# The first norm of a two-layer decoder trunk: which engine forms its shifts, scales and sums of squares, and how many weight tiles follow its channel blocks

## The chip, the cores and the metric

The kernel runs on one core of a Trainium2 chip. The metric is device time in microseconds (us), the median of three runs. Engines are named as in the profile: PE is TensorE's matrix multiply, PEld its weight load, DVE is VectorE, ACT is ScalarE, POOL is GpSimd, SP is the queue from which all DMAs here are issued.

## The reference

There are two layers over 256 tokens of 1024 channels. Each has a mixer and an expert channel mixer, both behind a norm whose shift and scale come from a conditioning vector `c`. What matters here is the start of layer 0:

```
c_act = silu(c)
sh1, sc1, ... = split(c_act @ ada_w[0] + ada_b[0], 6)
h = x * rsqrt(mean(x*x) + 1e-6) * g * (1 + sc1) + sh1
z = h @ w_in          # mLSTM q, k, gates, o; MoBA q, k (column tiles); both v (row tiles)
```

`h` has 1024 channels, `w_in` gives 21 column tiles of 128 outputs and 8 row tiles for the two values. Everything after this is the same before and after the change.

## The kernel before

All work is float32. Channels are cut in eight blocks `kd` of 128, with channels on partitions and 256 tokens along the free axis. A weight tile is 128 x 1024 (512 KB); `load` (L146) takes it through SP into one of eight `raw` buffers. `split` (L152) makes a high part `hi` on ACT (L159) and a remainder `lo` on DVE (L162); three pairs of such buffers exist in the pool `stream`. A column tile against `h` then costs three matmuls of 256 columns for each channel block (`hi` by `hhi`, `hi` by `hlo`, `lo` by `hhi`: L185 to L187), 24 in all, which add up in one PSUM bank. We call such a sum over one weight tile a *tile product*.

`setup` (L85) loads the small parameters and `x`, forms `cact = silu(c)`, and copies `cact` to all partitions with eight f32 matmuls (L133); the result is `crow`.

`mixer0` (L426) begins with the norm. `norm_stat` (L271) squares one channel block on ACT (L279) and adds it to a running sum on DVE (L281); after the eighth, two f32 matmuls against a column of ones (L290) give the sum of squares per token. `norm_rstd` (L296) takes the power -1/2 on POOL (L262) and spreads the result over partitions with two f32 matmuls (L306). DVE then multiplies `x` by it (L440): `xn`.

For each channel block, `ada` (L244) forms 128 scales and then 128 shifts. Each is one custom DVE instruction over a 128 x 1024 tile of `ada_w` (L252), a read of its accumulator, and for the scale a small product (L255). ACT applies scale and shift twice (L449 gives `hhi`, L450 a float32 copy), DVE subtracts (L451 gives `hlo`). At blocks 4, 5 and 7 (`EARLY`) the first three column tiles are loaded and split. `col_tiles` (L189) multiplies those three in a staggered order through `mm_col` (L174), then goes on tile by tile, with a row step (12 matmuls of 512 columns, L237 to L239) behind some of them (`ROWS0`).

Each finished tile product is read from PSUM at once: the gates by DVE (L570, L571), a q or k tile by one ACT instruction (L484) and three on DVE (L486). The first nine column tiles are one of gates and eight of q and k.

The order of each engine's instructions is fixed ahead of the run by a planner. It takes the instructions in program order of priority, places each when its own cost table says that the inputs are there, and so may interleave products of several blocks; on the chip each engine works through its list in that order. `issue_after` holds an instruction behind another. `keep_warm` (L264) issues matmuls of 512 columns whose result nobody reads.

Of the kernel before, what the change touches and what calls it, by code (L numbers as in the profile page):

```python
# [9 lines left out]
F32 = mybir.dt.float32  # L10
# [10 lines left out]
P = 128  # L21
# [29 lines left out]
SIDE_N = ((8, 24), (0, 8))  # L51
EARLY = (4, 5, 7)
V1_AT = 15
# [21 lines left out]
class Prog:  # L75
# [9 lines left out]
    def setup(self):  # L85
# [35 lines left out]
        c = self.small[:, Cols.c:Cols.c + 8]  # L121
        cact = self.tmp.tile([P, KD], F32, tag="t8b", name="cact")
        e = self.tmp.tile([P, KD], F32, tag="t8", name="c_exp")
# [5 lines left out]
        for half in range(2):  # L129
            ps = self.psum("h")  # L130
            for k in range(4):
                kd = 4 * half + k
                nc.tensor.matmul(ps[:, k * P:(k + 1) * P], lhsT=cact[:, kd:kd + 1].to_broadcast([P, P]), rhs=self.ident,  # L133
                                 start=True, stop=True)
            self.last_crow = nc.vector.tensor_copy(self.crow[:, 512 * half:512 * half + 512], ps)

# [14 lines left out]

    def split(self, raw, late=None):  # L152

        nc = self.nc
        hi = self.stream.tile([P, 1024], F32R, tag="hi", name="hi")
        lo = self.stream.tile([P, 1024], F32R, tag="lo", name="lo")

        def high():
            nc.scalar.copy(hi, raw)  # L159

        def low():
            self.last_lo = nc.vector.tensor_tensor(out=lo, in0=raw, in1=hi.bitcast(F32), op=ALU.subtract)  # L162

        for part, kd in zip((high, low), late or (None, None)):
            if kd is None:
                part()
            else:
                self.late.append((kd, part))
        return hi, lo
# [18 lines left out]

    def col_tiles(self, aps, act, tags, kds=range(KD), ws=None, rest=None):  # L189

        n = len(tags)
        ws = ws or [self.wsplit(a) for a in aps[:n]]
        pss = [self.psum(t)[:, :T] for t in tags]
        self.mm_col(pss, ws, act, kds)
        yield from enumerate(pss)
        for i, a in enumerate(aps[n:]):
            ps = self.psum(rest(n + i) if rest else "h")[:, :T]
            w = self.take(a)
            self.mm_col([ps], [w], act)
            yield n + i, ps  # L200
# [62 lines left out]

    def keep_warm(self, n):  # L264

        ps = self.psum("h")
        for i in range(n):
            self.nc.tensor.matmul(ps, lhsT=self.zero.to_broadcast([P, P]), start=True, stop=True,
                                  rhs=self.iota.unsqueeze(1).to_broadcast([P, 4, P]))
# [61 lines left out]
    def alibi(self, pool):  # L331

        nc = self.nc
        di = pool.tile([P, T], I32, tag="sm_p", name="dist_i", bufs=12)
        nc.gpsimd.iota(di, pattern=[[-1, T]], base=P, channel_multiplier=1)
        df = pool.tile([P, T], F32, name="dist_f")
        nc.vector.tensor_copy(df, di)
        nc.gpsimd.affine_select(df, df, pattern=[[-1, T]], base=P, channel_multiplier=1, compare_op=ALU.is_ge, fill=-NEG)
        return df, pool.tile([P, NH, T], F32, name="alibi")

# [85 lines left out]
    def mixer0(self):  # L426
        nc, tc = self.nc, self.tc
        with ExitStack() as st:
# [3 lines left out]
            hlo = self.hp.tile([P, KD, T], F32R, tag="x", name="hlo")  # L432
            with tc.issue_after(self.last_crow.ins):
                for kd in range(KD):
                    self.norm_stat(kd, (0, 0))
            r = self.norm_rstd()
            xn = pool.tile([P, KD, T], F32, tag="yhi", name="xn")
            for half in range(2):
                ks = slice(4 * half, 4 * half + 4)
                nc.vector.tensor_mul(xn[:, ks, :], self.xT[:, ks, :], r.unsqueeze(1).to_broadcast([P, 4, T]))  # L440
            ws = []
            for kd in range(KD):
                for _ in chain(self.ada(0, 1, (kd,)), self.ada(0, 0, (kd,))):
                    pass
                if kd in EARLY:
                    ws.append(self.wsplit(self.io["ev_in"][(12, 0, 1)[len(ws)]]))
                g, sh = self.gsc[:, 0, 0, kd:kd + 1], self.mod[:, 0, kd:kd + 1]
                t = self.tmp.tile([P, T], F32, tag="nt", name="ht")
                nc.scalar.activation(hhi[:, kd, :], xn[:, kd, :], AF.Identity, bias=sh, scale=g)  # L449
                nc.scalar.activation(t, xn[:, kd, :], AF.Identity, bias=sh, scale=g)  # L450
                nc.vector.tensor_tensor(out=hlo[:, kd, :], in0=t, in1=hhi[:, kd, :].bitcast(F32), op=ALU.subtract)  # L451
            h = (hhi, hlo)
            yhi = pool.tile([P, KD, T], F32R, tag="yhi", name="yhi")
            ylo = pool.tile([P, KD, T], F32R, name="ylo")
            w_in = self.io["ev_in"]
            live = []

            qk = pool.tile([P, 8, T], F32, name="qk")
            mo = pool.tile([P, 4, T], F32, name="mo")
            cols = [12] + list(range(8)) + [13, 17, 14, 18, 15, 19, 16, 20, 8, 9, 10, 11]  # L460
            mv = pool.tile([P, TT, 4, P + 1], F32, name="mv")
            nc.vector.memset(mv[:, :, :, P:], 1.0)
            bv = pool.tile([P, TT, 1, 512], F32, name="bv")
            rows = {}
            zs = []
            cols = [w_in[c] for c in cols]
            row_aps = [self.io["ev_v"][n, w4] for n in range(2) for w4 in range(4)]
            self.feed, n = [], 0
            for i in range(3, 21):
                self.feed.append(cols[i])  # L470
                self.feed += row_aps[n:n + ROWS0.get(i, 0)]
                n += ROWS0.get(i, 0)
# [3 lines left out]
            tag0 = lambda i: "t" if min(ROWS0) < i <= max(ROWS0) else "h"  # L476
            for i, ps in self.col_tiles(cols, h, ("h", "h", "l"), ws=ws, rest=tag0):
                if i == 0:
# [41 lines left out]
            while live:  # L520
                self.advance(live)
            yield from self.residual(0, 16, self.io["ev_out"], (yhi, ylo), (4, 5, 6, 0, 1, 2, 3, 7))

    def moba_pair(self, pool, hp, zs, bv, bias, yhi, ylo):
# [628 lines left out]
def layout(x, c, ada_w, ada_b, norm_mix_g, norm_ffn_g, ev_w_in, ev_conv_w, ev_igate_b, ev_fgate_b, ev_mnorm_g,  # L1153
# [12 lines left out]
    def cols(v):  # L1166
# [12 lines left out]
    w = np.asarray(ev_w_in)[0]  # L1179
    z = lambda n: np.zeros((D, n), w.dtype)  # L1180
    gates = np.concatenate([w[:, 2048:2052], z(28), w[:, 2052:2056], z(92)], axis=1)
    ev = np.concatenate([w[:, 0:1024], w[:, 1536:2048], gates, w[:, 2056:3080]], axis=1)
# [3 lines left out]
        "small": np.ascontiguousarray(small),  # L1186
        "ada_w": np.ascontiguousarray(np.asarray(ada_w).transpose(0, 2, 1)).reshape(2, 6, KD, P, D),
        "ev_in": coltiles(ev),
        "ev_v": rowtiles(np.concatenate([w[:, 1024:1536], w[:, 3080:3592]], axis=1)),
# [28 lines left out]
```

## Time and profile before

| | |
|---|---|
| median of 3 runs | 1979.51 us (1978.45 to 1979.65) |
| the profiled execution: time / span | 1977.66 us / 1975.9 us |
| PE busy | 1934.8 us (98%), 13229 matmul instructions |
| DVE busy | 1538.6 us (78%) |
| ACT busy | 1136.1 us (57%) |
| granted clock of PE, mean | 0.989 |

Busy time is the share of the span in which an engine had an instruction in flight. An f32 matmul shows as two instructions, called passes below, and a matmul's shown duration overlaps with the next one's, so the cost of one in a stream is the distance between starts. [...]

### The profile page before, as it was taken

How to read it: one execution, taken by the hardware profiler on the slowest of the kernel's cores; microseconds unless marked ns; L12 is line 12 of the kernel's file. 1: busy time of each engine (PE TensorE's matmuls, PEld its weight loads, DVE VectorE, ACT ScalarE, POOL GpSimd, SP SyncE). 2: the span in 40 equal slices, each digit the busy share in tenths (PEclk: the TensorE clock that was granted, in tenths of full speed). 3: DMA queues.
4: the chain of work that ended last, by engine and by line, in shares of the span. 5: the costliest groups of instructions: out<-in, count | busy, mean ns of one | idle time of the engine just before them, and what ended most of it. 6: DMA issues, size and time to landing. Idle time of an engine off the chain costs nothing.

```text
span 1975.9 us, 34938 instructions
## 1 busy us (share of the span) xinstructions
PE 1934.8 (98%) x13229; PEld 1754.6 (89%) x13229; DVE 1538.6 (78%) x3336; ACT 1136.1 (57%) x2137; POOL 50.7 (3%) x37
## 2 busy tenths in 40 slices
PE   5999999999999999999999999999999999999999
PEld 4888999999999888888878799999999998888887
DVE  8977999789998666777578789988899975556655
ACT  4655555778775444444456554567877744444443
POOL 0020000000000000000012100000000000000000
PEclk7999999999999999999989999999999999999999
DMA  9863355444445666998356243554544455669660
GB/s 338 290 207 130 108 178 188 162 160 160 164 155 173 210 216 219 336 342 299 129 197 206 72 138 119 184 180 153 166 156 162 160 180 192 193 197 359 225 200 22
DMA packets 103992, 376.45 MB, mean 191 GB/s; under 512 B 11536, under 2 KB 12944, under 8 KB 103696
## 3 DMA queue, kind: packets, MB, share of 16 engines
q1 hardware_dynamic: 103824, 374.22, 56.3%
q8 instruction: 104, 1.70, 0.3%
q14 instruction: 64, 0.52, 0.1%
HBM read 373.12 MB, written 1.05 MB: 189 GB/s over the span
## 4 chain that ended last, share of the span: by engine, by line
PE 79%; DVE 12%; issue 5%; DMA 2%; ACT 1%; POOL 0%; POOLq 0%; ACTq 0%; DVEq 0%; SPq 0%
PE ps_h L185 12%; PE ps_acc L920 12%; PE ps_acc L921 12%; PE ps_acc L919 12%; PE ps_h L186 11%; PE ps_h L187 11%; DVE lo L162 4%; PE ps_g L1109 3%; DVE raw L252 1%; DMA raw<-in_ada_w_dram 1%; PE ps_l L389 1%; DVE idxs L987 1%; DVE mr L985 1%; DVE A L1116 1%; DVE idxs L984 1%
## 5 line engine op out<-in xcount | busy, mean ns | idle before, releaser
L159 ACT CAST hi<-raw 128x1024 fp32r<-128x1024 f32 x613 | 643.2, 1050 | 658.1 <-PE ps_acc L920 308.2
L162 DVE TENSOR_TENSOR lo<-raw,hi 128x1024 fp32r<-128x1024 f32 x613 | 748.3, 1221 | 300.7 <-ACT hi L159 297.7
L185 PE MATMUL ps_h<-h2hi,hi 128*128 128x256 f32 x2256 | 652.8, 289 | 1.1 <-ACT A L967 0.7
L187 PE MATMUL ps_h<-h2hi,lo 128*128 128x256 f32 x2256 | 638.3, 283 | 0.0
L186 PE MATMUL ps_h<-h2lo,hi 128*128 128x256 f32 x2256 | 638.1, 283 | 0.0
L185 PEld LDWEIGHTS ps_h<-h2hi,hi 128*128 128x128 f32 x2256 | 432.1, 192 | 2.0 <-ACT A L967 1.2
L187 PEld LDWEIGHTS ps_h<-h2hi,lo 128*128 128x128 f32 x2256 | 432.3, 192 | 0.9 <-DVE lo L162 0.4
L186 PEld LDWEIGHTS ps_h<-h2lo,hi 128*128 128x128 f32 x2256 | 432.9, 192 | 0.0
L919 PE MATMUL ps_acc<-hi,act 128*128 128x512 f32 x1024 | 397.8, 389 | 2.0 <-ACT act L900 2.0
L920 PE MATMUL ps_acc<-hi,act 128*128 128x512 f32 x1024 | 398.6, 389 | 0.1
L921 PE MATMUL ps_acc<-lo,act 128*128 128x512 f32 x1024 | 398.6, 390 | 0.0
L919 PEld LDWEIGHTS ps_acc<-hi,act 128*128 128x128 f32 x1024 | 192.1, 188 | 41.8 <-ACT act L900 2.4
L920 PEld LDWEIGHTS ps_acc<-hi,act 128*128 128x128 f32 x1024 | 192.2, 188 | 40.8 <-DVE act L901 1.0
L921 PEld LDWEIGHTS ps_acc<-lo,act 128*128 128x128 f32 x1024 | 192.0, 188 | 40.5 <-DVE lo L162 0.3
L252 DVE CUSTOM_DVE_ANT_0 raw<-raw,crow,small 128x1024 f32<-128x1024 f32 x96 | 122.6, 1279 | 26.6 <-DMA raw<-in_ada_w_dram 26.6
L1116 DVE SCALAR_TENSOR_TENSOR A<-A,ps_g 128x256 f32<-128x256 f32 (+28 forms) x214 | 124.4, 582 | 11.9 <-PE ps_g L1109 11.1
L1118 ACT ACTIVATE A<-ps_g 128x256 f32<-128x256 f32 (+39 forms) x170 | 69.2, 446 | 76.0 <-DVE A L1116 75.0
L1096 DVE TENSOR_TENSOR og<-oj,gt 128x512 f16<-128x512 f16 x256 | 100.8, 419 | 13.3 <-PE ps_g L1109 13.1
L1083 ACT ACTIVATE oi<-iota,in 128x128 f16<-128x128 f16 x320 | 107.1, 394 | 0.0
L185 PE MATMUL ps_h<-hhi,hi 128*128 128x256 f32 x248 | 76.0, 308 | 7.4 <-ACT hhi L449 3.4
L1109 PE MATMUL ps_g<-oi,og 128*128 128x128 f16 x1024 | 81.8, 223 | 0.0
L901 DVE TENSOR_TENSOR act<-A,act 128x1024 fp32r<-128x1024 f32 x64 | 78.0, 1218 | 1.5 <-ACT act L900 1.5
(313 smaller groups left out, 2076.1 us busy)
## 6 DMA issues: line engine op xcount, KB each, us to landing
raw<-in_uT_dram SPq DMA_DIRECT2D x256, 512.0 KB, 3.5
raw<-in_v_dram SPq DMA_DIRECT2D x256, 512.0 KB, 4.4
raw<-in_ada_w_dram SPq DMA_DIRECT2D x96, 512.0 KB, 5.1
raw<-in_wq_dram SPq DMA_DIRECT2D x32, 512.0 KB, 3.7
raw<-in_ev_in_dram SPq DMA_DIRECT2D x21, 512.0 KB, 5.0
raw<-in_od_in_dram SPq DMA_DIRECT2D x16, 512.0 KB, 4.3
raw<-in_ev_v_dram SPq DMA_DIRECT2D x8, 512.0 KB, 4.9
raw<-in_ev_out_dram SPq DMA_DIRECT2D x8, 512.0 KB, 4.5
```

The lines of the kernel that those rows point to most:

```text
L159: nc.scalar.copy(hi, raw)
L162: self.last_lo = nc.vector.tensor_tensor(out=lo, in0=raw, in1=hi.bitcast(F32), op=ALU.subtract)
L185: nc.tensor.matmul(ps, lhsT=whi[:, s], rhs=ahi[:, kd, :], start=kd == kds[0], stop=False)
L186: nc.tensor.matmul(ps, lhsT=whi[:, s], rhs=alo[:, kd, :], start=False, stop=False)
L187: nc.tensor.matmul(ps, lhsT=wlo[:, s], rhs=ahi[:, kd, :], start=False, stop=kd == kds[-1])
L252: nc.vector.tensor_tensor_reduce(w, w, self.crow, 1.0, self.small[:, ab:ab + 1], ALU.mult, ALU.add, m)
L919: nc.tensor.matmul(acc[q], lhsT=xhi, rhs=vhi[:, c], start=m == 0, stop=False)
L920: nc.tensor.matmul(acc[q], lhsT=xlo, rhs=vhi[:, c], start=False, stop=False)
L921: nc.tensor.matmul(acc[q], lhsT=xhi, rhs=vlo[:, c], start=False, stop=m == NEXP - 1)
L1083: nc.scalar.activation(oi[:, k, :], self.iota, AF.Square, bias=tabs["in"][:, t0 + k:t0 + k + 1])
L1109: nc.tensor.matmul(pv[:, k, :], lhsT=og[:, w, :, k], rhs=oi[:, k, :], start=w == 0, stop=w == 1)
L1116: nc.vector.scalar_tensor_tensor(dst, dst, 1.0 / GSC, pv[:, :, lo:m], op0=ALU.mult, op1=ALU.mult)
```

## The change

The work before the first tile products moves to a new function, `first_blocks`.

- The eight shifts, and the scales of channel blocks 1, 3, 5 and 7, are formed on PE: eight f32 matmuls with a weight tile as stationary operand and one column of `cact` as the moving one. They read a second copy of the same weights, `ada0`, laid out by column tiles. DVE adds the bias from PSUM. The other four scales stay on DVE. All twelve results go to columns of one PSUM tile, `sums`.
- The squares stay on ACT; PE sums them, two f32 matmuls of one column for each channel block, in place of DVE's additions.
- Six column tiles, instead of three, are loaded early. Tile products take a channel block as soon as `h` has it; a tile that comes later catches up. The pairs of buffers of tiles 3 to 5 lie in the room of tiles that are used later.
- Six, four and three matmuls of `keep_warm` stand behind the columns of blocks 0, 1 and 2.
- The six finished products are then read in the old order, and the rest goes on as before.

```diff
@@ -49,7 +49,9 @@
-EARLY = (4, 5, 7)
+SC_PE = (1, 3, 5, 7)
+FIRST = {0: 1, 1: 2, 2: 1, 3: 1, 4: 1}
+WARM0 = {0: 6, 1: 4, 2: 3}
@@ -119,7 +121,7 @@
-        cact = self.tmp.tile([P, KD], F32, tag="t8b", name="cact")
+        self.cact = cact = const.tile([P, KD], F32, name="cact")
@@ -132,7 +134,7 @@
-            self.last_crow = nc.vector.tensor_copy(self.crow[:, 512 * half:512 * half + 512], ps)
+            nc.vector.tensor_copy(self.crow[:, 512 * half:512 * half + 512], ps)
@@ -149,11 +151,10 @@
-    def split(self, raw, late=None):
-
-        nc = self.nc
-        hi = self.stream.tile([P, 1024], F32R, tag="hi", name="hi")
-        lo = self.stream.tile([P, 1024], F32R, tag="lo", name="lo")
+    def split(self, raw, late=None, parts=None):
+        nc = self.nc
+        hi, lo = parts or [self.stream.tile([P, 1024], F32R, tag=t, name=t) for t in ("hi", "lo")]
@@ -186,12 +187,13 @@
-    def col_tiles(self, aps, act, tags, kds=range(KD), ws=None, rest=None):
-
-        n = len(tags)
-        ws = ws or [self.wsplit(a) for a in aps[:n]]
-        pss = [self.psum(t)[:, :T] for t in tags]
-        self.mm_col(pss, ws, act, kds)
+    def col_tiles(self, aps, act, tags, kds=range(KD), ws=None, rest=None, pss=None):
+        n = len(pss or tags)
+        if not pss:
+            ws = ws or [self.wsplit(a) for a in aps[:n]]
+            pss = [self.psum(t)[:, :T] for t in tags]
+            self.mm_col(pss, ws, act, kds)
@@ -261,9 +263,9 @@
-    def keep_warm(self, n):
-
-        ps = self.psum("h")
+    def keep_warm(self, n, ps=None):
+        ps = self.psum("h") if ps is None else ps
@@ -336,7 +338,7 @@
-        return df, pool.tile([P, NH, T], F32, name="alibi")
+        return df, pool.tile([P, NH, T], F32, tag="alibi", name="alibi")
@@ -430,51 +432,32 @@
-            with tc.issue_after(self.last_crow.ins):
-                for kd in range(KD):
-                    self.norm_stat(kd, (0, 0))
-            r = self.norm_rstd()
-            xn = pool.tile([P, KD, T], F32, tag="yhi", name="xn")
-            for half in range(2):
-                ks = slice(4 * half, 4 * half + 4)
-                nc.vector.tensor_mul(xn[:, ks, :], self.xT[:, ks, :], r.unsqueeze(1).to_broadcast([P, 4, T]))
-            ws = []
-            for kd in range(KD):
-                for _ in chain(self.ada(0, 1, (kd,)), self.ada(0, 0, (kd,))):
-                    pass
-                if kd in EARLY:
-                    ws.append(self.wsplit(self.io["ev_in"][(12, 0, 1)[len(ws)]]))
-                g, sh = self.gsc[:, 0, 0, kd:kd + 1], self.mod[:, 0, kd:kd + 1]
-                t = self.tmp.tile([P, T], F32, tag="nt", name="ht")
-                nc.scalar.activation(hhi[:, kd, :], xn[:, kd, :], AF.Identity, bias=sh, scale=g)
-                nc.scalar.activation(t, xn[:, kd, :], AF.Identity, bias=sh, scale=g)
-                nc.vector.tensor_tensor(out=hlo[:, kd, :], in0=t, in1=hhi[:, kd, :].bitcast(F32), op=ALU.subtract)
+            cols = [self.io["ev_in"][i] for i in [12] + list(range(8)) + [13, 17, 14, 18, 15, 19, 16, 20, 8, 9, 10, 11]]
+            pss = self.first_blocks(pool, (hhi, hlo), cols)
...
-            ylo = pool.tile([P, KD, T], F32R, name="ylo")
-            w_in = self.io["ev_in"]
+            ylo = pool.tile([P, KD, T], F32R, tag="ylo", name="ylo")
...
-            mo = pool.tile([P, 4, T], F32, name="mo")
-            cols = [12] + list(range(8)) + [13, 17, 14, 18, 15, 19, 16, 20, 8, 9, 10, 11]
+            mo = pool.tile([P, 4, T], F32, tag="mo", name="mo")
...
-            bv = pool.tile([P, TT, 1, 512], F32, name="bv")
+            bv = pool.tile([P, TT, 1, 512], F32, tag="bv", name="bv")
...
-            cols = [w_in[c] for c in cols]
...
-                self.feed.append(cols[i])
+                if i >= len(pss):
+                    self.feed.append(cols[i])
...
-            for i, ps in self.col_tiles(cols, h, ("h", "h", "l"), ws=ws, rest=tag0):
+            for i, ps in self.col_tiles(cols, h, (), rest=tag0, pss=pss):
@@ -521,6 +504,80 @@
+    def first_blocks(self, pool, h, cols):
+        nc, tc = self.nc, self.tc
+        hhi, hlo = h
+        one_b = pool.tile([P, KD], F32, name="one_b")
+        nc.vector.tensor_scalar_add(one_b, self.small[:, Cols.ada_b + 8:Cols.ada_b + 16], 1.0)
+        sums, warm = self.psum("t"), self.psum("l")
+        ssq = [self.psum("g") for _ in range(TT)]
+        for kd in range(KD):
+            sq = self.tmp.tile([P, T], F32, tag="nt", name="sq")
+            nc.scalar.activation(sq, self.xT[:, kd, :], AF.Square)
+            for tt in range(TT):
+                nc.tensor.matmul(ssq[tt][:, 0:1], lhsT=sq[:, tt * P:(tt + 1) * P], rhs=self.ones, start=kd == 0,
+                                 stop=kd == KD - 1)
+        v, rs = [self.tmp.tile([P, TT], F32, tag=t, name=t) for t in ("nv", "nr")]
+        for tt in range(TT):
+            nc.vector.tensor_scalar(v[:, tt:tt + 1], ssq[tt][:, 0:1], 1.0 / D, EPS, op0=ALU.mult, op1=ALU.add)
+        self.rsqrt(rs, v)
+        r = self.psum("t")[:, :T]
+        for tt in range(TT):
+            nc.tensor.matmul(r[:, tt * P:(tt + 1) * P], lhsT=rs[:, tt:tt + 1].to_broadcast([P, P]), rhs=self.ident,
+                             start=True, stop=True)
+        xn = pool.tile([P, KD, T], F32, tag="yhi", name="xn")
+        for half in range(2):
+            ks = slice(4 * half, 4 * half + 4)
+            nc.vector.tensor_mul(xn[:, ks, :], self.xT[:, ks, :], r.unsqueeze(1).to_broadcast([P, 4, T]))
+        def column(w, o):
+            for k in range(KD):
+                mm = nc.tensor.matmul(sums[:, o:o + 1], lhsT=w[:, k * P:(k + 1) * P], rhs=self.cact[:, k:k + 1],
+                                      start=k == 0, stop=k == KD - 1)
+            return mm
+        ws, pss, done = [], [], []
+        room = [None] * 3 + [pool.tile([P, 2, 1024], F32R, tag=t, name="first") for t in ("alibi", "ylo")]
+        room = [r and (r[:, 0], r[:, 1]) for r in room] + [
+            [pool.tile([P, 1024], F32R, tag=t, name="first") for t in ("mo", "bv")]]
+        def products(i, kd):
+            (whi, wlo), s = ws[i], slice(kd * P, (kd + 1) * P)
+            nc.tensor.matmul(pss[i], lhsT=whi[:, s], rhs=hhi[:, kd, :], start=kd == 0, stop=False)
+            nc.tensor.matmul(pss[i], lhsT=whi[:, s], rhs=hlo[:, kd, :], start=False, stop=False)
+            nc.tensor.matmul(pss[i], lhsT=wlo[:, s], rhs=hhi[:, kd, :], start=False, stop=kd == KD - 1)
+        for kd in range(KD):
+            m = self.mod[:, 0, kd:kd + 1]
+            mm = column(self.load(self.io["ada0"][kd]), kd)
+            nc.vector.tensor_add(m, sums[:, kd:kd + 1], self.small[:, Cols.ada_b + kd:Cols.ada_b + kd + 1])
+            if kd in SC_PE:
+                mm = column(self.load(self.io["ada0"][8 + kd]), 8 + kd)
+                nc.vector.scalar_tensor_tensor(self.gsc[:, 0, 0, kd:kd + 1], sums[:, 8 + kd:9 + kd], one_b[:, kd:kd + 1],
+                                               self.small[:, Cols.g_mix + kd:Cols.g_mix + kd + 1], op0=ALU.add, op1=ALU.mult)
+            else:
+                for _ in self.ada(0, 1, (kd,)):
+                    pass
+            if kd in WARM0:
+                with tc.issue_after(mm.ins):
+                    self.keep_warm(WARM0[kd], warm)
+            g = self.gsc[:, 0, 0, kd:kd + 1]
+            t = self.tmp.tile([P, T], F32, tag="nt", name="ht")
+            nc.scalar.activation(hhi[:, kd, :], xn[:, kd, :], AF.Identity, bias=m, scale=g)
+            nc.scalar.activation(t, xn[:, kd, :], AF.Identity, bias=m, scale=g)
+            nc.vector.tensor_tensor(out=hlo[:, kd, :], in0=t, in1=hhi[:, kd, :].bitcast(F32), op=ALU.subtract)
+            for i in range(len(ws)):
+                products(i, kd)
+            for _ in range(FIRST.get(kd, 0)):
+                i = len(ws)
+                ws.append(self.split(self.load(cols[i]), parts=room[i]))
+                pss.append(self.psum("hhllgg"[i])[:, :T])
+                for k in range(kd + 1):
+                    products(i, k)
+        return pss
@@ -1178,6 +1235,7 @@
+    a0 = np.asarray(ada_w)[0]
@@ -1185,6 +1243,7 @@
+        "ada0": coltiles(a0[:, 0:2 * D]),
```

## Rows read from the trace of the kernel before

**Rows 1.** Waits of PE, 0 to 80 us: total, times, longest us.
```profile
PE ps_g L290 <- DVE sqsum L281: 10.6, 1, 10.6
...
PE ps_h L185 <- ACT hhi L449: 3.4, 3, 1.9
...
PE ps_h L237 <- ACT sg L509: 0.8, 1, 0.8
```

**Rows 2.** Windows: stretch, length, busy us (x starts), clock, DMA share, GB/s.
```profile
9.50:10.00 0.50, 0.00 (x0) 0.90 0.97 401
...
37.00:37.50 0.50, 0.50 (x6) 0.79 0.89 328
...
7.00:43.48 36.48, 16.73 (x81) 0.63 0.95 361
43.48:50.00 6.52, 6.52 (x52) 1.00 0.85 296
...
7.00:41.00 34.00, 31.68 (x62) 0.60 0.96 365
```

**Rows 3.** The same view, L185 on PE alone.
```profile
7.00:43.48 36.48, 8.65 (x24) 0.63 0.95 361
```

**Rows 4.** Groups of DVE, 0 to 50 us: busy us, mean ns, idle before.
```profile
L252 DVE CUSTOM_DVE_ANT_0 raw<-raw,crow,small 128x1024 f32<-128x1024 f32 x16 | 20.4, 1278 | 0.0
L162 DVE TENSOR_TENSOR lo<-raw,hi 128x1024 fp32r<-128x1024 f32 x6 | 7.3, 1221 | 0.0
...
L281 DVE TENSOR_TENSOR sqsum<-sqsum,sq 128x256 f32<-128x256 f32 x7 | 2.9, 419 | 0.0
```

**Rows 5.** Timeline of PE, f32 passes and their neighbours: start us, us.
```profile
3.66 3.37 PE L133 MATMUL ps_h<-ident,cact 128*128 128x128 f32 x16 [3.66 <-DVE iota L113]
...
17.60 1.01 PE L290 MATMUL ps_g<-ones,sqsum 128*128 128x1 f32 x4 [10.57 <-DVE sqsum L281]
...
184.81 0.61 PE L290 MATMUL ps_g<-ones,sq 128*128 128x1 f32 x4
185.28 1.24 PE L268 MATMUL ps_h<-iota,zero 128*128 128x512 f16 x5
...
197.51 1.06 PE L974 MATMUL ps_acc<-keys,qry 128*128 128x128 f32 x8
198.32 0.36 PE L185 MATMUL ps_h<-h2hi,hi 128*128 128x256 f32 x1
```

**Rows 6.** Timeline of PE, idle matmuls and tile products at either clock.
```profile
183.57 0.82 PE L268 MATMUL ps_h<-iota,zero 128*128 128x512 f16 x3
184.23 0.50 PE L290 MATMUL ps_g<-ones,sqsum 128*128 128x1 f32 x4
...
35.12 0.41 PE L185 MATMUL ps_h<-hhi,hi 128*128 128x256 f32 x1
35.33 0.41 PE L186 MATMUL ps_h<-hlo,hi 128*128 128x256 f32 x1
...
44.22 0.28 PE L186 MATMUL ps_h<-hlo,hi 128*128 128x256 f32 x1
44.34 0.28 PE L187 MATMUL ps_h<-hhi,lo 128*128 128x256 f32 x1
```

**Rows 7.** Timeline: PE to DVE to ACT to PE; DVE reading finished products.
```profile
18.67 0.15 DVE L299 TENSOR_SCALAR nv<-ps_g 128x2 f32<-128x2 f32 x1
...
39.00 0.08 DVE L252 DVE_READ_ACCUMULATOR2_ANT mod<- 128x1 f32 x1
39.12 0.60 ACT L449 ACTIVATE hhi<-xn,mod,gsc 128x256 fp32r<-128x256 f32 x1 [1.77 <-DVE mod L252]
39.77 0.39 PE L185 MATMUL ps_h<-hhi,hi 128*128 128x256 f32 x1 [1.17 <-ACT hhi L449]
...
45.75 0.47 DVE L486 SCALAR_TENSOR_TENSOR qk<-ps_l,small,qk 128x255 f32<-128x255 f32 x1
46.14 0.47 DVE L486 SCALAR_TENSOR_TENSOR qk<-ps_h,small,qk 128x253 f32<-128x253 f32 x1
```

## The prediction

> **What bounds the kernel now.** I read the engine totals first: PE is busy for 98% of the span. PE is the only engine near its limit, so a change at the start can be worth only time in which PE does nothing useful. The waits of PE show where that is: 10.6 us for the sum of squares, 3.4 us for `hhi` [rows 1]. The windows give the whole stage. From 7.00 to 43.48 us PE's records cover 16.73 of 36.48 us, at a mean clock of 0.63; from 43.48 us on PE is dense, with one wait of 0.8 us for L237 [rows 1, 2]. Last I looked for what keeps PE waiting: DVE is busy for 31.68 of the 34 us up to 41.00, above all with sixteen 1.28 us reductions of `ada_w` [rows 2, 4]. So DVE bounds this stage, and PE bounds everything behind it.
>
> The question is therefore when PE has a given amount of useful work behind it. By 43.48 us it has done 24 starts of L185, three tile products [rows 3], and by 50.00 us 52 more matmuls [rows 2]. With the 72 of three products that is 124 of the 144 in six. If the new kernel has issued 124 of them before 50.0 us and stays dense, it is faster by the difference. All sums below are against the profiled execution, 1977.66 us; its span is 1975.9 us, and the remaining 1.76 us lie around it. The median of the runs is 1979.51 us, 1.85 us more, which I add at the end.
>
> **What the change takes from DVE.** Twelve reductions of 1.28 us, with the small instructions behind them, and seven additions of 0.42 us go, 15.4 + 2.9 and with the small ones some 19 us; three more `lo` of 1.22 us come earlier [rows 4]. DVE then has about 18 us of work in this stage and stops being its limit.
>
> **What it puts on PE.** PE is free at 7.03 us, when the copy of `cact` ends (3.66 + 3.37) [rows 5]. The trace has no column of `sums`, but it has the same instruction: f32 matmul, 128 x 128 stationary, one moving column. Two such matmuls appear as four passes. Where the clock is 1.00 four passes take 185.28 - 184.81 = 0.47 us, 0.12 each; passes with 128 moving columns take 0.81/8 = 0.10. At 0.50 the copy of `cact` took 3.37/16 = 0.21 each [rows 5]. One moving column is thus no cheaper than 128. I take 0.112 at the full clock and 0.21 at half.
>
> - Twelve sums of eight matmuls are 192 passes. Sixteen matmuls for the squares are 32, and the spreading of the root is 4. Together 228 passes, 25.5 us at the full clock and 47.9 us at half.
> - Thirteen `keep_warm` matmuls cost 0.66/3 = 0.22 us each [rows 6], 2.9 us.
> - 124 matmuls of tile products, 0.12 us apart at the full clock and 0.21 at half [rows 6], are 14.9 us or 26.
>
> The best case for PE, without one gap and all at the full clock, is 7.0 + 25.5 + 2.9 + 14.9 = 50.3 us. That is 0.3 us later than now. This is the core of my forecast: between 7.00 and 43.48 us PE gives 72 x 0.12 = 8.6 us to products and wastes 28 us today, and the new passes and idle matmuls cost it 25.5 + 2.9, the same. DVE is relieved, and PE takes over as the limit of the stage.
>
> [...]
>
> **What comes on top.** Clock: after the copy of `cact` ended at 7.03 us, with PE idle, the clock fell to 0.50 at about 9.9 us and came back only near 37.2 us, during dense tile products [rows 2, 5]. Whether passes with one column hold it, no row shows; bursts there are of four or eight. If all passes but not the products run at half, the price is 22.3 us; if the products do too, with idle matmuls at twice their price, about 36 us; if none does, nothing. I take 3 us: some 30 of the first 48 passes, those of the squares and of the first shift, which run before any idle matmul or product, at 0.10 us extra each. After that products are mixed in.
>
> Last block: behind the last sum stand DVE's addition (0.15 us), `hhi` and the eighteen products of channel block 7. From DVE's result at 39.08 to the first product at 39.77 us is 0.7 us now [rows 7]. I take 0.8 us; it is 2 us if DVE is in a 1.2 us instruction at that moment, and nothing if products of older blocks are left for the gap.
>
> Behind the six products: they all end within the last eighteen matmuls, 2.2 us. DVE then reads gates and five tiles, three instructions 0.39 us apart each [rows 7], some 7 us in a row, where now they come tile by tile. The first three pairs of `hi` and `lo` buffers also come free only there, and the row step needs the banks of products 0 and 1. PE's next weights queue behind these reads on DVE. A wait between nothing and 5 us; I take 1.2 us, since the first pair comes free some 1.8 us ahead of the end (15 matmuls of 0.12 us), in time for most of a split, whose `lo` takes 1.22 us [rows 4]. DMA costs nothing: eight buffers run ahead of PE at 410 GB/s [rows 2]; were they late, each load would cost 524/410 = 1.3 us.
>
> One bank: all twelve sums go to one PSUM tile which DVE reads between them. If PE may not write it while DVE reads, each sum waits for DVE's addition of the one before. The row for such a read: 0.06 us to its start at 18.67 us, 0.15 us long [rows 5, 7]. That is 0.3 us with the way back, eleven times 3.3 us, if nothing else is there for PE; with a 1.28 us instruction ahead on DVE each time, 17 us. Products of older blocks fill most of it, so I take 0.7 us.
>
> [...]
>
> Sum: 0.3 + 3.0 + 0.8 + 1.2 + 0.7 = 6.0 us. 1977.66 + 6.0 = 1983.7 us, and with 1.85 us for the median 1985.5 us.
>
> **Rivals.**
>
> *A, faster: a pass of one column is far cheaper in a long run of them.* Then PE isn't the limit but the loads are: 22 tiles of 0.524 MB, `x` and the parameters, 12.7 MB at 410 GB/s, are there at about 33 us; with the last hand-off and eighteen products six tile products end near 37 us instead of 52.4 (50.0 and twenty more matmuls). After 3 us for splits that aren't ready this is 12 us of gain, 1967.5 us. For it: DVE really is the limit today. Against it: every row of a pass, at one column or 128. [...] Chance 0.10.
>
> *B, no change: PE stays dense, the clock stays full, and the waits vanish among the products.* Then +0.3 us, perhaps -1 if the 0.8 us wait at L237 goes too: 1979 to 1981 us. For it: PE always has loaded work in this stage. Chance 0.22.
>
> *C, much slower: sums of one column leave the clock at half.* Between 7 and about 70 us all 228 passes cost 0.21 us: +22.3 us and half of the waits above, 2003 us; it decides as soon as more than about half of the passes run at 0.50. For it: the clock fell once PE's burst had ended [rows 2, 5]. Against: products and idle matmuls come between. Chance 0.13.
>
> *D, slower by the one bank:* PE waits at each sum for DVE, +10 us, 1990 us. Against: PE has products to do. Chance 0.07.
>
> **How the numbers follow.** A difference below 0.2%, 4 us, can't be told from none. The forecast has 0.48 with its own range of 1981 to 1990 us; a quarter of that lies within 4 us. Within 0.2%: 0.12 of it and 0.17 of B, 0.29. Slower: 0.36, C and D, 0.56. Faster: A and 0.05 of B, 0.15. The range reaches from between A and B, 1973 us, to the middle of C, 2003 us; it leaves out most of A and the worse half of C.
>
> **What would show it.** Right: PE without long gaps from 7 to 50 us, passes of the sums 0.11 to 0.12 us apart, the last sum behind 45 us, six products complete near 57 us, DVE idle for a third of the stage. The clock step is right if the rows show 0.50 only before about 17 us. Wrong: six products complete before 48 us, passes below 0.09 us, or sums that end when the loads do. A clock of 0.50 through the sums would be C, and gaps ahead of each sum that end at DVE's addition would be D.

## The result: slower by 1.8%, and the profile after

The changed kernel takes 2014.53 us (median of four runs, 2010.19 to 2018.05) against 1979.43 us; the ratio is 1.0181 [1.0163, 1.0198]. The forecast was 1985.5 us, with a range up to 2003. The profiled execution took 2010.19 us, its span is 2008.4 us, 32.5 more than before. It is the fastest of the four; by the medians the change costs 35.1 us. All stage times below are from profiled executions, one for each kernel.

The waits of PE, 0 to 110 us (total, times, longest), to be read against [rows 1]:

```profile
PE ps_g L520 <- ACT sq L518: 8.2, 4, 6.5
PE ps_g L657 <- DVE qk L469: 2.2, 1, 2.2
PE ps_t L528 <- POOL nr L264: 2.1, 1, 2.1
PE ps_h L548 <- ACT hhi L568: 1.9, 2, 0.9
...
PE ps_t L537 <- DVE gsc L558: 0.3, 1, 0.3
```

Waits do not explain 32 us: before, the sum of squares alone held PE for 10.6 us. The windows do; columns as in [rows 2], with PE, PEld, DVE, ACT and POOL in turn:

```profile
20.63:45.91 25.28, 25.28 (x110) 22.44 (x109) 9.00 (x15) 5.15 (x8) 0.00 (x0) 0.50 0.51 167
...
7.00:41.00 34.00, 30.13 (x139) 27.33 (x138) 11.34 (x21) 7.79 (x14) 1.68 (x1) 0.67 0.59 212
...
45.91:49.30 3.39, 3.39 (x32) 3.39 (x31) 0.16 (x1) 0.00 (x0) 0.00 (x0) 1.00 0.16 46
49.30:62.90 13.60, 12.66 (x58) 12.32 (x58) 4.62 (x9) 4.05 (x6) 0.00 (x0) 0.50 0.51 188
62.90:69.80 6.90, 6.59 (x59) 6.50 (x57) 0.80 (x3) 0.54 (x2) 0.00 (x0) 0.99 0.61 205
69.80:76.60 6.80, 6.80 (x34) 6.80 (x34) 1.85 (x5) 1.65 (x4) 0.00 (x0) 0.50 0.65 203
```

DVE fell from 31.68 to 11.34 us of the 34 us up to 41.00, and PE rose to 30.13. But from 20.63 to 45.91 us PE is busy without a gap at a granted clock of 0.50, half of the full one. It had fallen at 18.6 us, while PE waited for POOL. Behind 45.91 us it goes up and down by whole stretches. The timeline of PE shows both what holds the start back and what a pass costs (start us, us):

```profile
6.49 1.01 PE L520 MATMUL ps_g<-ones,sq 128*128 128x1 f32 x4 [6.49 <-ACT sq L518]
8.07 1.02 PE L520 MATMUL ps_g<-ones,sq 128*128 128x1 f32 x4 [0.57 <-ACT sq L518]
...
12.11 3.49 PE L135 MATMUL ps_h<-ident,cact 128*128 128x128 f32 x16
15.44 2.12 PE L520 MATMUL ps_g<-ones,sq 128*128 128x1 f32 x16
19.61 1.23 PE L528 MATMUL ps_t<-ident,nr 128*128 128x128 f32 x4 [2.05 <-POOL nr L264]
20.63 3.41 PE L537 MATMUL ps_t<-cact,raw 128*128 128x1 f32 x16
23.91 2.72 PE L270 MATMUL ps_l<-iota,zero 128*128 128x512 f16 x6
26.42 3.41 PE L537 MATMUL ps_t<-cact,raw 128*128 128x1 f32 x16
...
45.30 0.41 PE L549 MATMUL ps_l<-hlo,first 128*128 128x256 f32 x1
45.52 2.03 PE L537 MATMUL ps_t<-cact,raw 128*128 128x1 f32 x16
47.41 0.36 PE L550 MATMUL ps_l<-hhi,first 128*128 128x256 f32 x1
...
48.32 2.49 PE L537 MATMUL ps_t<-cact,raw 128*128 128x1 f32 x16
51.75 0.58 PE L548 MATMUL ps_h<-hhi,hi 128*128 128x256 f32 x1 [0.94 <-ACT hhi L568]
...
63.81 1.84 PE L537 MATMUL ps_t<-cact,raw 128*128 128x1 f32 x16
65.51 0.36 PE L550 MATMUL ps_g<-hhi,first 128*128 128x256 f32 x1
...
86.86 0.39 PE L239 MATMUL ps_h<-hi,hhi 128*128 128x512 f32 x1
...
94.25 0.37 PE L657 MATMUL ps_g<-ident,grow 4*128 4x4 f32 x2 [2.24 <-DVE qk L469]
```

The copy of `cact` now ends at 15.60 us (12.11 + 3.49) and not at 7.03 [rows 5], because the planner put four blocks' squares in front of it. The first sum starts at 20.63 us. Sixteen passes take (23.91 - 20.63)/16 = 0.205 us each there and (65.51 - 63.81)/16 = 0.106 at the full clock. (In the sum at 45.52 us they take 0.118, because the clock rises only at 45.9 us, shortly after its start.) Six idle matmuls behind the first sum take (26.42 - 23.91)/6 = 0.42 us each, twice their price in [rows 6], and the next sum is as slow as the first. At 45.9 us the clock has risen behind a run of tile products; at 49.4 us, within the sum that starts at 48.32, it falls again, with PE busy throughout. The six products are complete at 86.9 us; before, the same work was done at 52.4 us (50.0 and twenty matmuls). The sums of squares of the next norm mark the end of the mixer:

| | six products complete | end of first mixer | from there to the end of the span |
|---|---|---|---|
| before | 52.4 | 184.23 | 1791.7 |
| after | 86.9 (+34.5) | 222.00 (+37.8) | 1786.4 (-5.3) |

The last column was a surprise: no line of code behind the mixer had changed.

### The profile page after: what moved, and what is told of

It reads as the page before. It is cut to its first block, busy times and chain, and to the rows that moved or that the text cites. A ratio compares the mean times of both kernels' runs of the same rounds, so it can differ in the third digit from the quotient of the medians.

```text
span 2008.4 us, 35391 instructions
## 1 busy us (share of the span) xinstructions
PE 1967.6 (98%) x13462; PEld 1776.6 (88%) x13462; DVE 1524.2 (76%) x3315; ACT 1132.2 (56%) x2137; POOL 46.1 (2%) x37
## 4 chain that ended last, share of the span: by engine, by line
PE 74%; DVE 16%; issue 7%; ACT 2%; POOL 0%; DMA 0%; POOLq 0%; SPq 0%; ACTq 0%; DVEq 0%
PE ps_acc L978 11%; PE ps_acc L976 11%; PE ps_acc L977 11%; PE ps_h L186 9%; PE ps_h L188 9%; PE ps_h L187 9%; DVE lo L163 5%; DVE A L1173 2%; PE ps_g L1166 2%; PE ps_t L537 1%; DVE og L1153 1%; DVE mr L1042 1%; PE ps_l L391 1%; DVE idxs L1044 1%; PE ps_h L240 1%
## 5 line engine op out<-in xcount | busy, mean ns | idle before, releaser
L187 PE MATMUL ps_h<-h2lo,hi 128*128 128x256 f32 x2256 | 631.2, 280 | 0.0
L186 PEld LDWEIGHTS ps_h<-h2hi,hi 128*128 128x128 f32 x2256 | 424.9, 188 | 8.7 <-ACT A L1024 7.6
L188 PEld LDWEIGHTS ps_h<-h2hi,lo 128*128 128x128 f32 x2256 | 425.5, 189 | 3.7 <-DVE lo L163 3.3
L187 PEld LDWEIGHTS ps_h<-h2lo,hi 128*128 128x128 f32 x2256 | 428.0, 190 | 0.0
L254 DVE CUSTOM_DVE_ANT_0 raw<-raw,crow,small 128x1024 f32<-128x1024 f32 x84 | 107.5, 1279 | 19.9 <-DMA raw<-in_ada_w_dram 19.7
L1153 DVE TENSOR_TENSOR og<-oj,gt 128x512 f16<-128x512 f16 x256 | 101.0, 420 | 10.6 <-PE ps_g L1166 10.2
L1024 ACT ACTIVATE A<-ps_h 128x256 f32<-128x256 f32 (+38 forms) x238 | 72.2, 304 | 3.2 <-PE ps_h L188 3.1
```

Source lines behind the costliest of these rows:

```text
L186: nc.tensor.matmul(ps, lhsT=whi[:, s], rhs=ahi[:, kd, :], start=kd == kds[0], stop=False)
L187: nc.tensor.matmul(ps, lhsT=whi[:, s], rhs=alo[:, kd, :], start=False, stop=False)
L188: nc.tensor.matmul(ps, lhsT=wlo[:, s], rhs=ahi[:, kd, :], start=False, stop=kd == kds[-1])
L254: nc.vector.tensor_tensor_reduce(w, w, self.crow, 1.0, self.small[:, ab:ab + 1], ALU.mult, ALU.add, m)
L1153: nc.vector.tensor_tensor(out=og[:, w], in0=oj, in1=tabs["g"][:, w, ts].unsqueeze(1).to_broadcast(full), op=ALU.mult)
```

## The experiments

Theory: the cost is the half clock through the one-column sums (rival C) plus the late start of the sums. Rivals: the idle matmuls are the cost; a pass or a wait for DVE is simply dearer than forecast.

**One column or 128, same number of matmuls.** Each sum streams 128 equal columns, in four places of the bank:

```diff
-mm = nc.tensor.matmul(sums[:, o:o + 1], lhsT=w[:, k * P:(k + 1) * P], rhs=self.cact[:, k:k + 1],
...
+mm = nc.tensor.matmul(sums[:, o * P:(o + 1) * P], lhsT=w[:, k * P:(k + 1) * P],
+                      rhs=self.cact[:, k:k + 1].to_broadcast([P, P]), start=k == 0, stop=k == KD - 1)
...
```

> The changed kernel with 128 equal moving columns in each matmul of a sum instead of one, four places of 128 columns in the bank taken in turn; the number of passes is the same. [...] Rival 'work' (the passes themselves and the waits between them are the price, whatever the clock): passes cost as much or more, the time stays above 2005 us.

1992.73 us, ratio to before 1.0066 [1.0042, 1.009]; six products complete at 68.2 us. The clock theory had put the time at 1990 to 1998 us and the six products at 64 to 69 us; both hold. PE's timeline, the same stretch:

```profile
21.26 2.90 PE L537 MATMUL ps_t<-cact,raw 128*128 128x128 f32 x16
23.99 1.46 PE L270 MATMUL ps_l<-iota,zero 128*128 128x512 f16 x6
...
28.14 1.95 PE L537 MATMUL ps_t<-cact,raw 128*128 128x128 f32 x16
29.92 1.02 PE L270 MATMUL ps_l<-iota,zero 128*128 128x512 f16 x4
```

And its windows, PE alone:

```profile
20.00:30.00 10.00, 9.76 (x68) 0.84 0.68 212
30.00:40.00 10.00, 9.98 (x81) 1.00 0.97 344
```

It starts from nearly the same point, 21.26 us, with 2.0 us of idle PE ahead of the spreading of the root. Yet the clock is back at 1.00 at about 23.3 us and stays there until the six products are complete. The passes of the third sum are (29.92 - 28.14)/16 = 0.111 us apart, and the idle matmuls take 0.22 us. The edit also moves the results to other columns of the bank; that is hardly where the gain comes from, since the waits of these sums for DVE rose from 0.3 to 1.1 us. The same number of matmuls with 127 more columns each made the kernel 22 us faster. With one column PE had been busy too, for 25.28 of 25.28 us, but at 0.50.

**No idle matmuls:**

```diff
-WARM0 = {0: 6, 1: 4, 2: 3}
+WARM0 = {}
```

> The changed kernel without its thirteen idle matmuls. Theory 'clock': they run at 0.50 and don't raise it, so taking them away gives back 13 x 0.43 = 5.6 us, time 2005 to 2010 us. Rival 'the idle matmuls do hold the clock later on': without them the clock is at 0.50 for longer, time above 2016 us.

2011.44 us, 1.0166 [1.0145, 1.0186], six complete at 85.3 us. This lies between the two expectations, and its interval overlaps that of the changed kernel. What the thirteen idle matmuls cost or give back is too small to be told from nothing here.

**Sums of squares back on DVE**, behind the copy of `cact` as before:

```diff
-            nc.scalar.activation(sq, self.xT[:, kd, :], AF.Square)
-            for tt in range(TT):
-                nc.tensor.matmul(ssq[tt][:, 0:1], lhsT=sq[:, tt * P:(tt + 1) * P], rhs=self.ones, ...
...
+        with tc.issue_after(self.last_crow.ins):
+            for kd in range(KD):
+                self.norm_stat(kd, (0, 0))
+        r = self.norm_rstd()
```

> The changed kernel with the squares added up on DVE as before, behind the copy of cact; the sums of shifts and scales stay on PE with one column. Theory 'late start' (squares on PE push the copy of cact to 12.1 us and the first sum to 20.6 us, against 7.0 us at which PE was free before; 9 to 13 of the 34 us): first sum before 11 us, time 2001 to 2007 us. Rival 'the start does not matter, the last channel block waits for DMA or DVE': time above 2011 us.

1998.92 us, 1.0102 [1.0082, 1.0123], better than expected; six complete at 76.5 us. PE's timeline:

```profile
8.25 3.54 PE L526 MATMUL ps_t<-cact,raw 128*128 128x1 f32 x16 [8.25 <-DMA raw<-in_ada_dram]
11.66 3.76 PE L135 MATMUL ps_h<-ident,cact 128*128 128x128 f32 x16
15.21 2.00 PE L270 MATMUL ps_l<-iota,zero 128*128 128x512 f16 x6
17.04 1.84 PE L526 MATMUL ps_t<-cact,raw 128*128 128x1 f32 x16
```

The first sum starts at 8.25 us, as soon as its weights are there. The squares on PE had held it back by 12.4 us.

**Both repairs**, the two diffs above in one kernel:

> The changed kernel with both repairs: 128 equal moving columns in the sums, and the squares added up on DVE behind the copy of cact. If clock and late start are separate prices that add up, the six products end 10.4 us before the 68.2 us of the run with wide columns alone, at 56 to 59 us, and the time is 1980 to 1985 us: still not faster than before, because the passes fill what PE wasted (the floor of the prediction). Rival 'one cause' (late start and clock hang together, either repair gives the same): six products at 65 us or later, 1990 us or more. Rival 'the floor is wrong': below 1975 us.

1984.84 us, 1.0027 [1.0016, 1.0037]; six complete at 61.1 us, 8.7 us later than before. Its waits of PE, 0 to 70 us:

```profile
PE ps_g L646 <- DVE qk L469: 2.2, 1, 2.2
PE ps_h L537 <- ACT hhi L557: 1.4, 2, 0.9
PE ps_g L308 <- POOL nr L264: 1.2, 1, 1.2
PE ps_t L526 <- DVE mod L544: 1.0, 4, 0.3
```

**Squares on PE, but behind the copy of `cact`:**

```diff
-                nc.tensor.matmul(ssq[tt][:, 0:1], lhsT=sq[:, tt * P:(tt + 1) * P], rhs=self.ones, ...
+                with tc.issue_after(self.crow_mm.ins):
+                    nc.tensor.matmul(ssq[tt][:, 0:1], lhsT=sq[:, tt * P:(tt + 1) * P], rhs=self.ones, ...
```

> The changed kernel with one order altered: the squares' matmuls on PE stand behind the copy of cact (L135), as everything did before. Theory 'order' (the late start comes from squares at half clock that hand over to ACT one by one ahead of the copy): first sum at 14 to 16 us instead of 20.6, time 5 us less, 2005 to 2011 us. Rival 'the squares themselves': first sum still at 19 us or later, no gain.

2009.94 us, 1.0155 [1.0128, 1.0183]. The time is as expected, the mechanism is not: the first sum starts at 18.65 us, not at 14 to 16. The copy had cost only 2 us of the delay; the rest is the squares' own chain with ACT and POOL, in which 24 of their 32 passes now run at 0.21 us each. The clock takes another course too, which bears on the theory (PE's timeline, then windows with columns as in the first ones above):

```profile
21.93 2.72 PE L270 MATMUL ps_l<-iota,zero 128*128 128x512 f16 x6
24.44 2.02 PE L538 MATMUL ps_t<-cact,raw 128*128 128x1 f32 x16
...
26.75 2.19 PE L538 MATMUL ps_t<-cact,raw 128*128 128x1 f32 x16
```

```profile
20.50:24.44 3.94, 3.94 (x15) 2.47 (x14) 2.06 (x3) 1.09 (x2) 0.00 (x0) 0.50 0.30 93
25.00:28.00 3.00, 3.00 (x29) 3.00 (x28) 0.49 (x2) 0.00 (x0) 0.00 (x0) 1.00 0.18 34
28.50:31.50 3.00, 3.00 (x12) 2.18 (x12) 2.52 (x5) 2.03 (x3) 0.00 (x0) 0.50 0.99 389
```

Here the clock rises just behind the same six idle matmuls, between 24.44 and 25.00 us, and the second sum is fast, (26.32 - 24.44)/16 = 0.118 us a pass. It does not last: two one-column sums with three products between them keep PE busy without a gap, and between 28.0 and 28.5 us the clock falls. So in this run six idle matmuls were followed by the full clock, and it fell again within a one-column sum.

**What six tiles are worth with everything on DVE**, squares, shifts and scales, without idle matmuls:

```diff
-SC_PE = (1, 3, 5, 7)
+SH_PE = ()
+SC_PE = ()
-WARM0 = {0: 6, 1: 4, 2: 3}
+WARM0 = {}
...
+            if kd in SH_PE:
...
+            else:
+                for _ in self.ada(0, 0, (kd,)):
+                    pass
```

Then the same with the first four shifts as wide sums on PE, `SH_PE = (0, 1, 2, 3)`, and with four tiles, `FIRST = {0: 1, 1: 2, 2: 1}`.

> Six tile products by channel blocks alone: shifts, scales and squares on DVE as in the kernel before, no idle matmuls. Theory 'clock and PE work': this part of the change is good by itself; DVE bounds the stage with 3 x 1.22 us more for the lo parts, six products complete at about 47 us instead of 52.4, less 2 to 3 us of waits behind them: 1974 to 1978 us. Rival 'behind the six' (reading six products at once and splits that wait for their buffers cost as much as was won): 1979 us or more.

> Six tile products, squares on DVE, and only the shifts of channel blocks 0 to 3 on PE, with 128 equal moving columns, no idle matmuls: 64 passes in the 15 us in which PE idles anyway. DVE loses 4 x 1.5 us. If DVE still bounds the stage, the six products end 4 to 6 us before the 48.7 us of the run with six tiles alone: 1966 to 1971 us. Rival (PE passes land among the products, or DMA bounds it): 1971 us or more.

> As the run with six tile products alone, but with four: two lo parts fewer on DVE in the stage and five instead of seven us of reads behind it. If the waits behind the six products (2.2 us for the gates' transposes, 1.6 and 0.9 us for lo) come from the number of products read at once, they shrink and the time is 1968 to 1972 us; if the work on PE before the last channel block counts for more, 1974 to 1977 us.

1972.51 us, 0.9973 [0.996, 0.9985]; 1972.58 us, 0.9964 [0.9947, 0.9982]; 1975.86 us, 0.9984 [0.9974, 0.9993]. The first is below the expected 1974 to 1978 us and beats both kernels. The other two came out as their rivals had it: shifts on PE add nothing, and with four tiles PE's waits for `lo` do not shrink, one of them takes 3.7 us. But the mixer of the first ends at 184.22 us, as before; its whole gain lies behind the mixer, where all these variants are 4 to 7 us shorter. So I asked what else had moved. The change puts `cact`, 32 bytes in each partition, into another pool. By the compiler's addresses, which the expectations below give and no trace shows, this moves the weight tiles up by 32 bytes and the activation tiles down by 32.

**`cact` moved alone, in the kernel before, and moved back in two variants:**

```diff
-        cact = self.tmp.tile([P, KD], F32, tag="t8b", name="cact")
+        cact = const.tile([P, KD], F32, name="cact")
```

> The kernel before with one edit: cact lies in the constant pool, as in the changed kernel, and not in the temporary one. This moves the weight tiles up by 32 bytes in each partition (31968 to 32000) and the activation tiles hhi, hlo, h2hi, h2lo down by 32 (72160 to 72128); no instruction is added, removed or reordered. Theory (place): the stretch behind the first mixer is 4 to 7 us shorter in every six-tile variant because its 256-column products stand 0.1178 us apart and not 0.1200, and that comes from where the tiles lie: this kernel then takes 1973 to 1976 us with L185 at 286 ns mean instead of 289. Rival (order): it comes from the order of instructions that the six tiles leave behind: 1978.5 to 1980 us and 289 ns, as the kernel before.

> The six-tile variant with all sums and squares on VectorE (1972.51 us), with one edit: cact goes back to the temporary pool, so that every tile lies where the kernel before has it. Theory (place): it loses the 5 us and takes 1976 to 1979.5 us, 256-column products at 0.1200 us, so that six tiles in themselves give nothing or up to 3 us. Rival (order): it stays at 1971 to 1974 us.

> The changed kernel with cact back in the temporary pool, so that weight tiles and activations lie where the kernel before has them (31968 and 72160); the work is unchanged. If the changed kernel's shorter stretch behind the first mixer (1786.4 us from the end of the mixer to the end of the span, against 1791.7) is due to the place alone, as in the pair of six-tile variants, this takes 2018 to 2025 us, with 289 ns for the later products, and the change as such costs 40 us or more. If the order of instructions gives it, 2010 to 2016 us.

| kernel | `cact` in | us | ratio to before | first mixer ends | behind it |
|---|---|---|---|---|---|
| before | tmp | 1977.84 | | 184.23 | 1791.7 |
| before, moved | const | 1968.70 | 0.9958 [0.9944, 0.9971] | 185.97 | 1778.4 |
| six tiles | const | 1972.51 | 0.9973 [0.996, 0.9985] | 184.22 | 1785.2 |
| six tiles, moved back | tmp | 1980.73 | 1.0014 [1.0005, 1.0023] | 185.85 | 1794.2 |
| after | const | 2014.53 | 1.0181 [1.0163, 1.0198] | 222.00 | 1786.4 |
| after, moved back | tmp | 2017.84 | 1.0207 [1.0174, 1.024] | 223.11 | 1793.1 |

(Each ratio is to runs of the kernel before beside it; their medians lay between 1977.84 and 1979.43 us.) In all three pairs the stretch behind the mixer is longer by 7 to 13 us with `cact` in tmp. So the gain there belongs to the place. In the first two pairs the whole times confirm it, clear of each other; the first came out under the 1973 to 1976 us expected, the second above the 1976 to 1979.5. In the third pair they do not: the medians are 3.3 us apart and the intervals overlap, and the profiled execution of the changed kernel lies 4.3 us under its median, so part of its 1786.4 us may be luck. The last run's median is 0.2 us under the interval expected for place, and 289 ns is as expected.

The first of the three groups of the later 256-column products (busy us, mean ns, idle before), in the kernel before:

```profile
L185 PE MATMUL ps_h<-h2hi,hi 128*128 128x256 f32 x2256 | 652.8, 289 | 1.1 <-ACT A L967 0.7
```

The same group in that kernel with `cact` moved:

```profile
L185 PE MATMUL ps_h<-h2hi,hi 128*128 128x256 f32 x2256 | 643.3, 285 | 5.7 <-ACT A L967 4.7
```

And in the changed kernel with `cact` moved back:

```profile
L186 PE MATMUL ps_h<-h2hi,hi 128*128 128x256 f32 x2256 | 653.0, 289 | 2.7 <-ACT A L1024 2.4
```

The place alone takes 4 ns from each, and putting it back restores them (287 ns in the changed kernel as it was). A shown duration (0.28 us there) overlaps with the next one, so the spacing tells what that is worth: at about 227 us starts are 0.120 us apart in the kernel before and 0.114 with `cact` moved. Over the whole run the three groups of products show 29.5 us less, the three groups of 512-column matmuls in the expert stage 7.2 us more, and the stretch behind the mixer is 13.3 us shorter; the difference is not broken down. Six tiles by themselves, at the old place, cost 0.14%.

**Which operand's place?** A small pool ahead of the activations moves only these, or leaves only these where they were:

```diff
+        pad = ctx.enter_context(tc.tile_pool(name="pad", bufs=1, reuse_waits="tile")).tile([P, KD], F32, name="pad")
...
-        cact = self.tmp.tile([P, KD], F32, tag="t8b", name="cact")
+        cact = pad
```

The second has the pad, filled by one small memset, and `cact` in the constant pool.

> The kernel before with cact in a small pool of its own between the temporary pool and the activations: the activations hhi, hlo, h2hi, h2lo, which the products stream, move down by 32 bytes (72160 to 72128, a multiple of 64), the weight tiles stay at 31968 (32 above a multiple of 64). If it is the place of the streamed operand that makes the products closer, this takes 1973 to 1976 us with L185 at 286 ns; if it is that of the weights, 1978.5 to 1980 us and 289 ns.

> The counterpart: the weight tiles move up by 32 bytes (31968 to 32000), the activations stay at 72160 behind a pad of 32 bytes that one small memset fills. If it is the place of the weights, 1973 to 1976 us with L185 at 286 ns; if it is that of the streamed operand, 1978.5 to 1980 us and 289 ns.

Neither. Moved alone, each makes the kernel slower: 1990.64 us, 1.0062 [1.0048, 1.0076], and 1991.01 us, 1.0064 [1.0051, 1.0078]. One group of 512-column matmuls of the expert stage, in the kernel before and with the activations moved:

```profile
L920 PE MATMUL ps_acc<-hi,act 128*128 128x512 f32 x1024 | 398.6, 389 | 0.1
L921 PE MATMUL ps_acc<-hi,act 128*128 128x512 f32 x1024 | 404.7, 395 | 0.1
```

In both runs the three groups of products still show 12 to 13 us less than in the kernel before (288 ns for the first), but the three of the expert stage show 18.3 us more.

## Why the prediction was wrong

The direction was right and the size was not: +6.0 us forecast, +32.5 measured in the profiled spans (+35.1 by the medians). By its steps:

- **Clock, "I take 3 us": the step that failed.** It assumed that one-column passes, once mixed with products and idle matmuls, run at the full clock. The trace has 0.50 from 18.6 to 45.9 us and again for 13.6, 6.8 and 3.4 us before the six products are complete. With 128 columns they are complete 18.7 us earlier (86.9 to 68.2). Rival C named this and decided as it said, "as soon as more than about half of the passes run at 0.50": by their spacing 118 of the 228 did. I gave it 0.13, by counting the products and idle matmuls as cover that no row showed. C's 22.3 us is near these 18.7 by luck: it counts passes alone, all of them, where half of the passes and many products and idle matmuls were slow. So is the nearness of the prediction's "about 36 us" to the +34.5 us found, of which the late start, below, is a part.
- **"PE is free at 7.03 us."** The best case let 228 passes begin there without a gap. The squares' passes wait for ACT, block by block: 8.07 - 6.49 = 1.58 us each for the first four. They came ahead of the copy of `cact` on PE, and POOL's power then holds PE for 2.1 us. With the squares on DVE the first sum starts 12.4 us earlier and the six products are complete 10.4 us earlier. I counted these instructions' price but not the chain they stand in. "DMA costs nothing" was nearly right: without that chain the first sum waits for its weights until 7.79 or 8.25 us. (The 410 GB/s beside it is not in [rows 2], whose highest is 401; the trace before shows 410 from 6.50 to 7.00 us. The sum does not use it.)
- **The floor of the passes: right.** 0.106 us each at the full clock and 0.205 at half, against 0.112 and 0.21; 0.111 with 128 columns in the third sum. (The 0.21 is that of the copy of `cact` [rows 5], for which the profile shows 1.00; the first change it shows is at 9.9 us, to 0.50. That the copy ran at 0.50 was my estimate, from its pace.) With 0.106 in a run of sixteen, rival A is out.
- **Last block and one bank, 0.8 and 0.7 us.** That PE may not write the bank while DVE reads it was my assumption, and no run shows it or the 0.7 us by itself. The sums waited once for DVE's reading, 0.3 us; products filled the rest, so D is out. `hhi` held PE twice, for 1.9 us in all, once in mid-stage at 51.75 us. With both repairs the six products stand at +8.7 us, against +4.8 forecast (6.0 without the 1.2 behind them). Waits for `hhi`, POOL, `mod` and `gsc` come to 3.9 us there, 2.4 more than the 1.5 of these two terms; the first sum starts at 7.79 and not 7.03 us, which is 0.8; the last 0.7 us are not broken down.
- **Behind the six products, "I take 1.2 us": too small.** The shortfall grows from 34.5 to 37.8 us up to the mixer's end, 3.3 us, and by 2.3 to 5.1 us in the other variants on six tiles. PE's transposes of the gates (L657) wait 2.2 us for DVE, which reads q and k tiles, and the split's `lo` comes 0.9 us late. I had put up to 5 us in the bounds.
- **Not forecast: the move of `cact`**, -5.3 us behind the mixer in the profiled executions. Because of it the 1984.84 us with both repairs, which looks like the forecast, is not a hit: its mixer ends 13.3 us late, and the place gives 5 of that back. At the old place the change costs 38.9 us in the mixer (223.11 - 184.23).

What stays open: what made PE's clock fall under one-column sums (the runs show only that it fell, at 49.4 us and, with the squares behind the copy, between 28.0 and 28.5 us, that it stayed at 1.00 through the sum at 63.81 us, and that with 128 columns it was 1.00 from about 23.3 to 68.2 us), and why the place matters. Both moves together helped (0.9958), each alone harmed (1.0062 and 1.0064), and the kernel before and the six-tile variant with the same offsets differ (285 and 286 ns, 1778.4 and 1785.2 us). Of the after kernel's 25.8 us that the two repairs return together, 3.3 us are counted in both single runs (18.7 + 10.4 = 29.1).

## What to carry over

Before moving work to an engine, look for a row in which that engine keeps its clock on this very shape of instruction; cover that no row shows is no cover, and when the clock dropped here, everything mixed in paid too: 0.42 us and not 0.22 for an idle matmul, 0.21 and not 0.12 for a matmul of a tile product. Count where a moved step's first instruction can start, not only what its instructions cost. When a stretch that nobody edited changes its time, compare the addresses of its tiles: the kernel before with one 32-byte tile in another pool, 1968.70 us, has the lowest median of all that ran.

## What the runs showed of the hardware that was not expected

- PE was busy for all of 25.28 us at a granted clock of 0.50, and the clock fell from 1.00 to 0.50 with PE busy without a gap (at 49.4 us in the changed kernel, between 28.0 and 28.5 us with the squares behind the copy). With 128 equal columns instead of one it stayed at 1.00 from about 23.3 us until the six products were complete, and the passes took about as long as those of one column at the full clock: 0.111 us against 0.106 (0.205 at half).
- Six idle matmuls of 512 columns stood between the first two one-column sums, and the second was as slow as the first (0.42 us each, 2.5 us in all); the clock rose only at 45.9 us, behind a run of tile products. With the squares behind the copy the same six were followed by a rise, between 24.44 and 25.00 us. So six of them came before a rise in one run and not in the other.
- Moving `cact` to the other pool (by the compiler's addresses, weight tiles by 32 bytes and activations by -32 bytes in each partition) changed the mean of the 256-column products from 289 to 285 ns, and the whole kernel by 0.42%; either move alone cost 0.6%.
